# A decoder trunk on one core: the low weight parts of two Conformer layers made by accumulating DMA, with the convolution work divided anew

## The chip, the core and the metric

The kernel runs on one NeuronCore of a Trainium2 chip. A core has a matrix engine (PE, with its weight loads shown apart as PEld), a vector engine (DVE), an activation engine (ACT), a general engine (POOL) and a queue engine (SP) that issues transfers; 16 DMA engines move the data. The five engines run their own instruction lists in order and wait for one another through semaphores. The metric is the device time of one execution in microseconds, lower being better.

## The reference: what is computed

Four residual layers over a sequence of 512 positions with 1024 channels, in the order Conformer, forgetting attention, short convolution, Conformer. Each adds its mixer's output to the stream. Only the two Conformer layers (layer 0 and layer 3) change here:

```python
def conformer_conv_mixer(h, w_in, conv_w, conv_b, ln_g, ln_b, w_out):
    proj = h @ w_in                                  # 1024 -> 3 x 2048
    val, glu_gate, z = jnp.split(proj, 3, axis=-1)
    u = val * jax.nn.sigmoid(glu_gate)
    u = causal_depthwise_conv(u, conv_w) + conv_b    # 31 taps for each of 2048 channels
    u = jax.nn.silu(layer_norm(u, ln_g, ln_b))       # mean and variance over all 2048 channels
    return (u * jax.nn.silu(z)) @ w_out              # 2048 -> 1024
```

The layer norm runs over all channels, so every channel's convolution must be finished before the first value can enter the output projection. All inputs are float32.

## The kernel before

**Precision.** The matmuls run on float32r operands. To keep float32's accuracy each operand is split into a high part (the value cast to float32r) and a low part (the value less its high part), and a product is the sum of three matmuls: high by high, high by low, low by high.

**Weights.** All weights come as 289 chunks of 128x1024 (512 KB). A Conformer layer uses 64: 48 for the input projection (`val`, `gate` and `z` for each of 16 tiles of 128 channels) and 16 for the output projection. For each chunk SP loads `w_raw`, ACT casts it to `w_hi` (L315), and in a Conformer layer POOL subtracts to get `w_lo` (L413); in the output projection DVE may do it too. Three `w_raw` buffers and four pairs of `w_hi` and `w_lo` are in rotation, so the chunk three ahead is prepared while PE works. One chunk is 24 matmuls of 128x512.

**The convolution.** Tile i of u has 31 taps. Tap 0 is an ACT copy into the PSUM tile `cv`. Some taps go to the side: ACT multiplies u by the tap's weight (`prod`, L317) and POOL adds it to `pacc` (L330); `POOL_TAPS` holds how many taps a tile gives away. The rest are DVE instructions (L341, `cv<-u,vt,cv`), one for each tap, each reading the one before. At the end DVE adds `cv`, bias and `pacc` into `d`. Tiles in `PE_TILES` are done by PE instead: ACT reorders u into four phases (`ua`), SP writes it to DRAM (`ud`) and reads it back in four pieces (`phases`), 36 matmuls with banded matrices `pw` give `cv`, ACT copies it (`oa`), SP takes it through DRAM again (`od`, `ob`), and ACT puts it in order into `d`.

**Statistics.** POOL keeps running sums `s1` (of `d`) and `s2` (of its square, `sq`). The last two tiles, 14 and 15, don't go through POOL: PE adds their columns to the sum over channels directly, in PSUM tiles `meanp` and `e2p`. From those come `mean` and `var`, the inverse root `lnrp`, and then for each tile k the gated value (`make_g`: subtract the mean, multiply by `lnrp`, Silu on ACT, multiply by `sz`), split into `g_hi` (ACT) and `g_lo` (DVE). PE's output projection (`o`) takes them two tiles to a chunk.

**Order.** The program registers operations in a list (`Plan`), with a cost for each engine that may run it, and `Plan.trace` simulates the engines by those costs and emits the instructions in the order that comes out; each engine then runs its list in that order. Priorities are the position in the list plus `boost`. The costs are a plan, not measured times. `z` projections are registered nine tiles behind `val` and `gate` (`LAG`), and PE fills its time with them: an order on PE is free of the convolution until the statistics.

```python
POOL_TAPS = (0, 7, 7, 7, 7, 7, 7, 7, 7, 7, 7, 7, 7, 7, 9, 7)
PE_TILES = {0: (7, 12, 15), 3: (7, 12, 15)}
```

**Start.** In layer 0, x arrives in eight pieces, ACT makes `hh` and the squares `sq` of each, PE projects the first four chunks with unnormalised inputs, and sums the squares with a matrix of ones (`ms`); the inverse root `rstd` then gives the normalised `hn` for the other chunks.

Of the kernel before, what the change touches and what calls it, by code (L numbers as in the profile page):

```python
# [16 lines left out]
P = 128  # L17
# [72 lines left out]
class Op:  # L90
    __slots__ = ("engines", "fn", "prio", "table", "deps", "after", "unmet", "ready", "start",
                 "bufs", "new", "urgent")


class Plan:
# [23 lines left out]
    def op(self, engines, fn, r=(), w=(), boost=0, table=None):  # L119

        o = Op()
        o.engines, o.fn, o.prio, o.table = engines, fn, len(self.ops) + boost, table
        o.urgent = boost <= -2000 and "dma" not in engines
# [23 lines left out]
    def trace(self, switch):  # L147
# [25 lines left out]
        for _ in range(len(ops)):  # L173
# [57 lines left out]
            for m in o.after:  # L231
# [3 lines left out]
                if len(p.engines) > 1 or e not in p.engines:  # L235
                    late = self.LATENCY + (self.SLACK if "pe" in p.engines else 0.0)
# [14 lines left out]
def trunk(ctx: ExitStack, tc: tile.TileContext, x, w, vec, pw, out):  # L251
# [38 lines left out]
    def dve_time(n, fast=False):  # L290
        return 0.16 + n * (0.52e-3 if fast else 1.042e-3)
# [111 lines left out]
    def split_chunk():  # L403
# [5 lines left out]
        act(hi, raw, None, cost=1.03, boost=-600)  # L409
# [5 lines left out]
        parts[n] = hi, lo  # L415
        state["split"] += 1
# [26 lines left out]
    memset(ones_d, 1.0 / D)  # L443
    memset(ones_e, 1.0 / E)
# [39 lines left out]
    class Stream:  # L484
# [8 lines left out]
        def add(self, d):  # L493
# [7 lines left out]
            act(sq, xs[d], AF.Square, boost=40 if self.layer == 0 else 0)  # L501
# [24 lines left out]
    def out_projection(layer, gh, gl, make_g, banks):  # L526
# [5 lines left out]
        def evac(d, acc):  # L532
            tt(("dve",), xs[d], acc, xs[d], A.add)
            if last_layer:
                plan.op({"dma": 0.9}, lambda e, d=d: nc.sync.dma_start(out[d], xs[d]()), [xs[d]])
            else:
                nxt.add(d)

# [28 lines left out]
    def conformer(layer, st):  # L567
# [3 lines left out]
        raw_tiles, SPREAD, SHIFTED, DIRECT = 2, 12, 4, 2  # L571
# [3 lines left out]

        s1, s2, m0 = slot("s1"), slot("s2"), slot("m0")
# [34 lines left out]
        def conv_pe(i):  # L611
# [10 lines left out]
            def swap(src, dram, dst):  # L622

                plan.op({"dma": 2.5}, lambda e: nc.sync.dma_start(dram(), src()), [src], [dram], first)
                for k in range(NP):
# [3 lines left out]
                        [dram], [dst], first)  # L629

            plan.op({"act": 0.65}, lambda e: nc.scalar.copy(
                ua()[:, :].rearrange("p (h m) -> p h m", h=NP),
                u()[:, :].rearrange("p (m h) -> p h m", h=NP)), [u], [ua], first)
            swap(ua, ud, r)
            jobs = [(g, lag) for g in range(NP) for lag in range(NL)]
            for k in range(0, len(jobs), 4):
                mats = slot("pw", ring=("pw", 5))
                plan.op({"dma": 0.8}, lambda e, mats=mats, k=k: nc.sync.dma_start(
                    mats(), pw[n if layer == 0 else len(PE_TILES[0]) + n, k // 4]), w=[mats])
# [5 lines left out]
            act(oa, acc, None, boost=first)  # L645
# [396 lines left out]
```

## Time and profile before

| what | value |
|---|---|
| runs shown | 1792.42, 1793.99, 1795.02 us; median 1793.99 |
| the profiled execution | 1794.22 us, of which the trace spans 1792.3 |
| PE | 1767.3 us busy (99%), 8196 matmuls |
| DVE, POOL, ACT | 1167.2 (65%), 1096.9 (61%), 866.7 us (48%) |
| layer 0 | from the start to about 402.7 us |
| layer 3 | from 1400.3 us to the end |
| DMA | 182.4 MB, mean 102 GB/s |

The trace is one execution. Its groups give, for each line, engine and pair of tiles, how many instructions there were, their busy time and mean length, and the idle time just before them with what ended it. Matmuls are pipelined: one matmul's shown length (389 ns) overlaps the next, so PE's speed is read from the start-to-start time of a run of them, in the chain of waits, and a PE that shows as busy may still be waiting inside. An fp32 matmul is recorded as two entries. The share of an engine over the whole span hides that DVE and POOL are loaded in the Conformer layers far above their averages.

### The profile page before, as it was taken

To read this page: it belongs to the slowest core of one execution; us is meant where nothing else is said; L and a number is where in the kernel's file an instruction comes from. 1 tells how busy PE (TensorE), PEld (TensorE's weight loads), DVE (VectorE), ACT (ScalarE), POOL (GpSimd) and SP (SyncE) were. 2 spreads that over 40 slices of the span, in tenths; PEclk is the share of its full clock that TensorE was granted. 3 is DMA by queue.
4 is the path that set the end of the run, shared out by engine and by line. 5 is a ranking of instruction groups with operands and counts; after the bars stand their busy time and mean duration, and the time that the engine had idled before them with its cause. 6 is when DMAs were issued, how large, how long until landed. Compare 5 with 4: busy or idle time off the path is not lost.

```text
span 1792.3 us, 21883 instructions
## 1 busy us (share of the span) xinstructions
PE 1767.3 (99%) x8196; PEld 1462.4 (82%) x8196; DVE 1167.2 (65%) x1690; ACT 866.7 (48%) x1255; POOL 1096.9 (61%) x654
## 2 busy tenths in 40 slices
PE   8999999999999999999999999999999999999999
PEld 6788887888888888888788888888888878878787
DVE  6999997736777777867523333333313699999770
ACT  6656655536555555656433222222223564755550
POOL 5999998865333333544454555455445599989882
PEclk9999999999999999999999999999999999999999
DMA  6243432233222222222222222222223224334222
GB/s 219 83 154 99 141 135 83 94 106 118 83 78 91 85 77 85 75 77 71 71 95 94 94 94 100 101 94 95 96 100 123 88 94 147 106 129 136 94 94 71
DMA packets 63065, 182.40 MB, mean 102 GB/s; under 512 B 7136, under 2 KB 13280, under 8 KB 62960
## 3 DMA queue, kind: packets, MB, share of 16 engines
q1 hardware_dynamic: 62960, 181.02, 29.9%
q8 instruction: 64, 1.05, 0.2%
q14 instruction: 41, 0.34, 0.1%
HBM read 175.71 MB, written 5.28 MB: 101 GB/s over the span
## 4 chain that ended last, share of the span: by engine, by line
PE 81%; DVE 16%; POOL 1%; issue 1%; DMA 1%; ACT 0%; SPq 0%; DVEq 0%; POOLq 0%; ACTq 0%
PE o L379 19%; PE z L379 17%; DVE cv L341 13%; PE k L379 5%; PE v L379 5%; PE u L379 5%; PE c L379 5%; PE b L379 5%; PE q L379 5%; PE gate L379 3%; PE val L379 3%; PE cv L379 2%; PE op L379 2%; PE lg L379 2%; PE pt L874 1%
## 5 line engine op out<-in xcount | busy, mean ns | idle before, releaser
L413 POOL TENSOR_TENSOR w_lo<-w_raw,w_hi 128x1024 fp32r<-128x1024 f32 x274 | 661.1, 2414 | 586.2 <-PE z L379 110.0
L315 ACT CAST w_hi<-w_raw 128x1024 fp32r<-128x1024 f32 x289 | 303.2, 1050 | 550.9 <-issue 137.1
L341 DVE SCALAR_TENSOR_TENSOR cv<-u,vt,cv 128x495 f32<-128x495 f32 (+24 forms) x608 | 447.2, 736 | 19.7
L330 POOL TENSOR_TENSOR pacc<-prod,pacc 128x510 f32<-128x510 f32 (+5 forms) x148 | 174.7, 1181 | 11.1 <-ACT prod L317 4.4
L330 DVE TENSOR_TENSOR x<-o,x 128x512 f32<-128x512 f32 x32 | 21.2, 687 | 200.9 <-PE o L379 200.9
L317 ACT ACTIVATE prod<-u,vt 128x510 f32<-128x510 f32 (+8 forms) x166 | 106.9, 709 | 46.3 <-DVE u L330 46.3
L379 PE MATMUL o<-g_hi,w_hi 128*128 128x512 f32 x512 | 127.9, 391 | 0.7 <-DVE z L330 0.7
L379 PE MATMUL o<-g_lo,w_hi 128*128 128x512 f32 x512 | 127.0, 389 | 0.0
L379 PE MATMUL o<-g_hi,w_lo 128*128 128x512 f32 x512 | 126.7, 389 | 0.0
L379 PEld LDWEIGHTS o<-g_hi,w_hi 128*128 128x128 f32 x512 | 95.8, 188 | 21.7 <-DVE z L330 1.5
L379 PEld LDWEIGHTS o<-g_hi,w_lo 128*128 128x128 f32 x512 | 96.0, 188 | 19.9
L379 PEld LDWEIGHTS o<-g_lo,w_hi 128*128 128x128 f32 x512 | 95.9, 188 | 19.8
L246 ACT ACT_TABLE_LOAD x70 | 89.8, 1283 | 1.9 <-PEq L1030 0.7
L330 DVE TENSOR_TENSOR z<-z,rstd 128x512 f32<-128x512 f32 x32 | 22.1, 691 | 90.2 <-PE z L379 90.1
L379 PE MATMUL z<-hn_hi,w_hi 128*128 128x512 f32 x256 | 65.8, 400 | 2.2 <-ACT sz L317 2.2
L379 PE MATMUL z<-hl,w_hi 128*128 128x512 f32 x256 | 64.6, 394 | 0.0
L379 PE MATMUL z<-hn_hi,w_lo 128*128 128x512 f32 x256 | 64.3, 393 | 0.0
L379 PE MATMUL z<-hh,w_hi 128*128 128x512 f32 x256 | 64.0, 392 | 0.0
L379 PE MATMUL z<-hn_lo,w_hi 128*128 128x512 f32 x256 | 63.7, 391 | 0.0
L379 PE MATMUL z<-hh,w_lo 128*128 128x512 f32 x256 | 63.3, 389 | 0.0
L379 PEld LDWEIGHTS z<-hn_hi,w_hi 128*128 128x128 f32 x256 | 48.1, 191 | 13.9 <-ACT sz L317 3.8
L341 DVE SCALAR_TENSOR_TENSOR hl<-x,vt,hh 128x512 fp32r<-128x512 f32 x32 | 47.6, 1508 | 16.6 <-ACT hh L317 16.6
(245 smaller groups left out, 3708.1 us busy)
## 6 DMA issues: line engine op xcount, KB each, us to landing
w_raw<-w SPq DMA_DIRECT2D x289, 512.0 KB, 3.3
pw<-pw SPq DMA_DIRECT2D x54, 256.0 KB, 4.5
nc<-cd SPq DMA_DIRECT2D x16, 256.0 KB, 3.6
x<-x SPq DMA_DIRECT2D x8, 256.0 KB, 5.2
out<-x SPq DMA_DIRECT2D x8, 256.0 KB, 3.7
ud<-ua SPq DMA_DIRECT2D x6, 256.0 KB, 2.0
phases<-ud SPq DMA_DIRECT2D x24, 64.0 KB, 2.5
od<-oa SPq DMA_DIRECT2D x6, 256.0 KB, 3.9
```

Source lines behind the costliest of these rows:

```text
L246: switch(table)
L315: nc.scalar.copy(of(dst, d), of(src, s))
L317: nc.scalar.activation(of(dst, d), of(src, s), func, **kw)
L330: eng[e].tensor_tensor(of(dst, d), of(a, s), of(b, sb), op)
L341: nc.vector.scalar_tensor_tensor(of(dst, d), of(a, s), c, bb.bitcast(F32) if b_f32r else bb, op0, op1)
L379: nc.tensor.matmul(o, a, b, start=start, stop=stop)
L413: eng[e].tensor_tensor(lo(), raw(), hi().bitcast(F32), A.subtract)
L874: nc.tensor.transpose(tp()[:, blk(i - j)], p[i]()[:, blk(j)], ident())
```

## The change

In chunks 9 to 55 (layer 0) and 234 to 280 (layer 3), 47 in each layer, `w_lo` is made another way: ACT writes the negated high part into `w_lo`, and POOL issues a DMA that reads the weights from DRAM a second time and adds them into `w_lo` in place. After the middle of the output projection the old way is used again. The PE convolution tiles go from 7, 12 and 15 to 8 and 15; the other tiles give 9 taps to POOL instead of 7 (tile 14: 10 instead of 9). Only the last DVE tile (14) is added to the statistics directly by PE; tile 15 now goes through POOL's running sums. The DMAs to DRAM of a PE tile are issued by ACT, right behind its copy, instead of SP. At the start, PE multiplies a matrix of ones by itself 11 times, DVE casts the first chunk, and POOL makes four of the eight squares. In layer 3 each output tile is added and stored in two halves. The planner gets a `lag` for transfers, and `sz` a higher priority.

```diff
+WARM = 11
-POOL_TAPS = (0, 7, 7, 7, 7, 7, 7, 7, 7, 7, 7, 7, 7, 7, 9, 7)
-PE_TILES = {0: (7, 12, 15), 3: (7, 12, 15)}
+POOL_TAPS = (0, 9, 9, 9, 9, 9, 9, 9, 9, 9, 9, 9, 9, 9, 10, 9)
+PE_TILES = {0: (8, 15), 3: (8, 15)}
...
-                    late = self.LATENCY + (self.SLACK if "pe" in p.engines else 0.0)
+                    late = self.LATENCY + o.lag + (self.SLACK if "pe" in p.engines else 0.0)
...
     def split_chunk():
...
-        act(hi, raw, None, cost=1.03, boost=-600)
+        if n == 0:
+            plan.op({"dve": 0.7}, lambda e: nc.vector.tensor_copy(hi(), raw()), [raw], [hi], -600)
+        else:
+            act(hi, raw, None, cost=1.03, boost=-600)
+        parts[n] = hi, lo
+        state["split"] += 1
+        if lo_engines["now"] == ("swdge",):
+            act(lo, hi, AF.Copy, scale=-1.0, cost=1.05, boost=-600)
+            plan.op({"pool": 0.9}, lambda e: nc.gpsimd.dma_start(lo(), w[n], accum_op=A.add),
+                    [hi], [lo], boost=-600, lag=5.5)
+            return
...
+    warm = psum("o", "warm")
+    mms(lambda: [(warm()[:, :P], ones_d(), ones_d(), True, True)] * WARM, [warm], 0.4 * WARM,
+        [ones_d], -3000)
...
-            act(sq, xs[d], AF.Square, boost=40 if self.layer == 0 else 0)
+            if self.layer == 0 and d % 2:
+                tt(("pool",), sq, xs[d], xs[d], A.mult)
+            else:
+                act(sq, xs[d], AF.Square, boost=40 if self.layer == 0 else 0)
...
+            y = [plan.buf(lambda: xs[d]()) for _ in range(2)]
+            for b, s in zip(y, (slice(0, T // 2), slice(T // 2, T))):
+                plan.op({"dve": dve_time(T // 2)}, lambda e, s=s: nc.vector.tensor_tensor(
+                    xs[d]()[:, s], acc()[:, s], xs[d]()[:, s], A.add), [acc, xs[d]], [b])
+                plan.op({"dma": 0.5}, lambda e, s=s: nc.sync.dma_start(
+                    out[d][:, s], xs[d]()[:, s]), [b])
...
+            def phases_out(e):
+                nc.scalar.copy(ua()[:, :].rearrange("p (h m) -> p h m", h=NP),
+                               u()[:, :].rearrange("p (m h) -> p h m", h=NP))
+                nc.scalar.dma_start(ud(), ua())
+            plan.op({"act": 1.05}, phases_out, [u], [ua, ud], first, lag=3.0)
+            swap(ud, r)
...
-            if i < NE - DIRECT:
+            if i != late:
                 tt(("pool",), s1, s1, d2[i], A.add)
                 tt(("pool",), s2, s2, sq, A.add)
...
+            if n == 6:
+                lo_engines["now"] = ("swdge",)
...
-                act(sz[i], acc, AF.Silu)
+                act(sz[i], acc, AF.Silu, boost=-300)
...
-        lo_engines["now"] = ("pool", "dve")
+        lo_engines["now"] = ("swdge",)
 
         def make_g(k):
+            if k == NE // 2:
+                lo_engines["now"] = ("pool", "dve")
```

The new order on two engines, at three places. First POOL's list in the middle of layer 0's convolutions, before (`w_lo23` is chunk 23's low part, `pacc` the running sum of one tile's side taps, `prod` ACT's product for a tap, with the width left by its shift; `m0` is a common offset, `d4` tile 4's result):

```order
L585 COPY pacc_164_1281<-m0_47_665 128x1
L330 TENSOR_TENSOR pacc_164_1281<-prod_165_952,m0_47_665 128x511
L413 TENSOR_TENSOR w_lo23_1292<-w_raw23_1123,w_hi23_1279 128x1024
L330 TENSOR_TENSOR pacc_164_1281<-prod_166_955,pacc_164_1281 128x510
L330 TENSOR_TENSOR pacc_164_1281<-prod_167_961,pacc_164_1281 128x509
L330 TENSOR_TENSOR s1_45_715<-s1_45_715,d4_143_1325 128x512
L330 TENSOR_TENSOR s2_46_717<-s2_46_717,sq_144_1341 128x512
L413 TENSOR_TENSOR w_lo24_1377<-w_raw24_1162,w_hi24_1356 128x1024
L330 TENSOR_TENSOR pacc_164_1281<-prod_168_977,pacc_164_1281 128x508
```

The same stretch of POOL's list now:

```order
L332 TENSOR_TENSOR pacc_175_1265<-prod_176_1098,m0_48_700 128x511
L332 TENSOR_TENSOR pacc_175_1265<-prod_177_1102,pacc_175_1265 128x510
L332 TENSOR_TENSOR pacc_175_1265<-prod_178_1106,pacc_175_1265 128x509
L332 TENSOR_TENSOR pacc_175_1265<-prod_179_1121,pacc_175_1265 128x508
L419 DMA w_lo23_1302<-w 128x1024
L332 TENSOR_TENSOR pacc_175_1265<-prod_180_1136,pacc_175_1265 128x507
L332 TENSOR_TENSOR s1_46_721<-s1_46_721,d4_152_1324 128x512
L332 TENSOR_TENSOR pacc_175_1265<-prod_181_1151,pacc_175_1265 128x506
L332 TENSOR_TENSOR s2_47_723<-s2_47_723,sq_153_1354 128x512
L419 DMA w_lo24_1358<-w 128x1024
```

Each subtraction over a chunk has become a DMA issue at about the same place, and more taps stand between two of them.

Second, PE's list in layer 0 where the statistics are closed, before (`z0_12` is the z projection of tile 12, `d14` and `d15` the last two convolution results; behind the last of the four statistics matmuls there are 80 matmuls of z until the first `o`):

```order
L379 MATMUL z0_12_351_2656<-hn0_7_lo_77_427,w_hi44_2433 128x512
L379 MATMUL meanp_359_2560<-d14_315_2669,ones_e_11_75 128x512
L379 MATMUL e2p_360_2568<-sq_316_2679,ones_e_11_75 128x512
L379 MATMUL meanp_359_2560<-d15_324_2565,ones_e_11_75 128x512
L379 MATMUL e2p_360_2568<-sq_338_2598,ones_e_11_75 128x512
L379 MATMUL z0_12_351_2656<-hn0_0_hi_55_276,w_lo44_2522 128x512
```

And now, with 64 matmuls of z behind it until the first `o`:

```order
L381 MATMUL z0_13_374_2763<-hn0_7_hi_77_411,w_hi45_2588 128x512
L381 MATMUL meanp_380_2784<-s1_46_721,ones_e_11_75 128x512
L381 MATMUL e2p_381_2786<-s2_47_723,ones_e_11_75 128x512
L381 MATMUL meanp_380_2784<-d14_336_2775,ones_e_11_75 128x512
L381 MATMUL e2p_381_2786<-sq_337_2782,ones_e_11_75 128x512
L381 MATMUL z0_13_374_2763<-hn0_0_lo_57_280,w_hi45_2588 128x512
```

The running sums, which PE took 64 matmuls of z earlier before, now stand directly ahead of tile 14, and one third of z tile 13's chunk and all of tile 12's lie before the statistics.

Third, PE's list at the same point of layer 3, where before the four matmuls stood together as in layer 0, again with 80 of z behind them. Now the two that close the statistics are eight matmuls of z apart; the second of them, and the two sides of it:

```order
L381 MATMUL z3_13_1808_14051<-hn3_5_lo_1506_11672,w_hi270_13866 128x512
L381 MATMUL z3_13_1808_14051<-hn3_6_lo_1509_11686,w_hi270_13866 128x512
L381 MATMUL z3_13_1808_14051<-hn3_7_lo_1512_11702,w_hi270_13866 128x512
L381 MATMUL e2p_1815_14034<-sq_1771_14067,ones_e_11_75 128x512
L381 MATMUL z3_13_1808_14051<-hn3_0_hi_1490_11563,w_lo270_13913 128x512
```

Behind it 56 matmuls of z are left until the first `o`.

More of the change, by code (lines that the diff above doesn't have):

```diff
@@ L117, in buf, with op @@
         return b
-    def op(self, engines, fn, r=(), w=(), boost=0, table=None):
+    def op(self, engines, fn, r=(), w=(), boost=0, table=None, lag=0.0):
         o = Op()
         o.engines, o.fn, o.prio, o.table = engines, fn, len(self.ops) + boost, table
+        o.lag = lag
         o.urgent = boost <= -2000 and "dma" not in engines
@@ L414, in split_chunk @@
         plan.op({e: cost[e] for e in lo_engines["now"]}, fn, [raw, hi], [lo], boost=-300)
-        parts[n] = hi, lo
-        state["split"] += 1
     def chunk():
@@ L532, in evac @@
         def evac(d, acc):
[L533 to L536, printed above, removed]
+            if not last_layer:
+                tt(("dve",), xs[d], acc, xs[d], A.add)
                 nxt.add(d)
+                return
+            y = [plan.buf(lambda: xs[d]()) for _ in range(2)]
[4 more added lines that the diff above has]
+                    out[d][:, s], xs[d]()[:, s]), [b])
         accs = [psum(banks[d], f"o{d}") for d in range(half)]
@@ L570, in conformer @@
         FIRST, EARLY = 2, 7
-        raw_tiles, SPREAD, SHIFTED, DIRECT = 2, 12, 4, 2
+        raw_tiles, SPREAD, SHIFTED = 2, 12, 4
         def cw(i, s):
             return v(f"conv_w{layer}", i * KC + KC - 1 - s)
+        late = max(i for i in range(NE) if i not in on_pe)
         s1, s2, m0 = slot("s1"), slot("s2"), slot("m0")
@@ L620, in conv_pe, with swap @@
                       for nm in (f"ud{layer}_{i}", f"od{layer}_{i}"))
-            def swap(src, dram, dst):
-                plan.op({"dma": 2.5}, lambda e: nc.sync.dma_start(dram(), src()), [src], [dram], first)
+            def swap(dram, dst):
                 for k in range(NP):
@@ L638, in conv_pe @@
                 plan.op({"dma": 0.8}, lambda e, mats=mats, k=k: nc.sync.dma_start(
-                    mats(), pw[n if layer == 0 else len(PE_TILES[0]) + n, k // 4]), w=[mats])
+                    mats(), pw[n if layer == 0 else len(PE_TILES[0]) + n, k // 4]), w=[mats],
+                    lag=4.0)
                 mms(lambda mats=mats, k=k: [
@@ L644, in conv_pe, with conv_out @@
                     [acc], 0.87, [mats, r], boost=first or SPREAD * (k // 4))
-            act(oa, acc, None, boost=first)
-            swap(oa, od, ob)
+            def conv_out(e):
+                nc.scalar.copy(oa(), acc())
+                nc.scalar.dma_start(od(), oa())
+            plan.op({"act": 1.05}, conv_out, [acc], [oa, od], first, lag=3.0)
+            swap(od, ob)
             vb, at = v(f"conv_b{layer}", i)
@@ L707, in conformer @@
                 sz[i] = slot(f"sz{i}")
-                act(sz[i], acc, AF.Silu)
+                act(sz[i], acc, AF.Silu, boost=-300)
         mp, ep = psum("o", "meanp"), psum("sum", "e2p")
-        for n, (a, b) in enumerate(zip([s1] + [d2[i] for i in range(NE - DIRECT, NE)],
-                                       [s2] + last)):
+        for n, (a, b) in enumerate(zip([s1, d2[late]], [s2] + last)):
             for dst, src in ((mp, a), (ep, b)):
                 mms(lambda n=n, dst=dst, src=src: [
-                    (dst(), ones_e(), src(), n == 0, n == DIRECT)], [dst], 0.86, [ones_e, src],
+                    (dst(), ones_e(), src(), n == 0, n == 1)], [dst], 0.86, [ones_e, src],
                     boost=-2000)
```

8 lines of the change are left out of this document (2 added, 6 removed).

## The prediction

> **What bounds the kernel now.** The page's first part first, then its chain of what ended last.
>
> ```profile
> PE 1767.3 (99%) x8196; PEld 1462.4 (82%) x8196; DVE 1167.2 (65%) x1690; ACT 866.7 (48%) x1255; POOL 1096.9 (61%) x654
> ```
>
> By this line PE bounds everything. I therefore cut out the stretches that the change touches: start, the convolutions of layer 0, its statistics, the convolutions of layer 3 (columns: stretch, length, busy time of PE, PEld, DVE, ACT, POOL, granted clock, DMA share, GB/s).
>
> ```profile
> 0.00:20.00 20.00, 13.20 (x30) 6.89 (x30) 8.65 (x8) 14.67 (x22) 11.81 (x20) 1.00 0.78 281
> 33.30:291.60 258.30, 253.94 (x1215) 210.90 (x1214) 246.32 (x343) 156.04 (x212) 236.66 (x168) 1.00 0.36 119
> 291.60:316.00 24.40, 24.40 (x102) 18.88 (x101) 15.65 (x23) 16.29 (x22) 17.71 (x12) 1.00 0.22 74
> 1430.00:1683.00 253.00, 247.09 (x1178) 205.42 (x1176) 235.24 (x326) 149.28 (x201) 231.47 (x165) 0.99 0.36 119
> ```
>
> In the convolutions three engines are nearly full: PE 253.9, DVE 246.3 and POOL 236.7 of 258.3. Which one sets the end shows in the groups of that stretch (count | busy, mean ns | idle before, and on whom) and in DVE's waits (us in all, count, longest).
>
> ```profile
> L341 DVE SCALAR_TENSOR_TENSOR cv<-u,vt,cv 128x501 f32<-128x501 f32 (+24 forms) x304 | 223.6, 736 | 9.8
> L341 DVE SCALAR_TENSOR_TENSOR d<-cv,vt,pacc 128x512 f32<-128x512 f32 x12 | 9.0, 750 | 2.0 <-DVE cv L341 0.7 <-POOL pacc L330 0.5
> L413 POOL TENSOR_TENSOR w_lo<-w_raw,w_hi 128x1024 fp32r<-128x1024 f32 x42 | 100.8, 2401 | 8.7 <-ACT w_hi L315 5.3 <-ACT hn_hi L315 2.6 <-issue 0.7
> L330 POOL TENSOR_TENSOR pacc<-prod,pacc 128x510 f32<-128x510 f32 (+3 forms) x74 | 87.3, 1181 | 5.6 <-ACT prod L317 2.4
> L330 POOL TENSOR_TENSOR s<-s,d 128x512 f32<-128x512 f32 x13 | 16.8, 1293 | 6.9 <-DVE d L341 6.7
> L330 POOL TENSOR_TENSOR pacc<-prod,m 128x511 f32<-128x511 f32 x9 | 9.8, 1091 | 0.0
> L317 ACT ACTIVATE prod<-u,vt 128x510 f32<-128x510 f32 (+7 forms) x83 | 53.2, 709 | 25.5 <-DVE u L330 25.5
> L315 ACT CAST w_hi<-w_raw 128x1024 fp32r<-128x1024 f32 x42 | 43.8, 1044 | 27.1 <-issue 14.2 <-PE z L379 8.1 <-PE gate L379 4.0
> ```
> ```profile
> DVE d L341 <- DVE cv L341: 0.7, 2, 0.5
> DVE d L341 <- POOL pacc L330: 0.5, 1, 0.5
> ```
>
> DVE is the bound: 304 taps with 9.8 us of idle before them, 0.03 us each with no releaser named, and almost nothing else that it waits for. PE is full only because z work, free of the convolution, fills it. When DVE's last tap is done the layer goes through statistics, and PE keeps busy with the z that was left over. Four numbers set the length of a Conformer layer: when DVE begins, how long its chain is, how long the last convolution takes to reach the last sum, and how long PE's z lasts behind it.
>
> ```profile
> 22.79 5.44 PE gate L379 x24
> 1648.37 8.03 PE cv L379 x72
> ```
>
> One chunk costs PE 5.44 us (0.2267 for a matmul), one PE convolution tile 8.03.
>
> **The change part by part.** *PE.* One PE tile and two pairs of sums (0.86 for a sum by start to start, below) less: 8.03 + 1.7 = 9.75 us in each layer. In the convolutions this is not on the path by itself. It makes room for 16 and 24 z matmuls ahead of the statistics, whose effect comes below.
>
> *DVE's chain.* Tiles 7 and 12 come to DVE (21 taps each), tile 8 leaves, and two taps of every other tile go to POOL: by the list of instructions 302 taps instead of 304, one more `d`. So -2 x 0.736 + 0.75 = -0.7 in a layer, **-1.4** in both.
>
> *POOL.* 39 passes of 2.40 in the stretch go, 39 DMA issues of unknown cost c come, with 31 more `pacc` adds (1.181), one `prod,m` (1.09), and one running-sum add net (1.29): 236.7 - 93.6 + 36.6 + 1.1 + 1.3 = 182.1 + 39c. No row of before shows c. It lies between SP's issue, in the tail row below (0.33), and POOL's own pass (2.40); I take 1.0, nearer to SP's because an issue touches no data of the tile. POOL then has 221 us of work in 257, less than before; with c up to 1.9 it fits. Cost nothing, then, hidden under DVE's taps.
>
> ```profile
> L366 DVE TENSOR_TENSOR hn_lo<-hn,hn_hi 128x512 fp32r<-128x512 f32 x5 | 3.3, 683 | 0.0
> L366 DVE TENSOR_TENSOR g_lo<-d,g_hi 128x512 fp32r<-128x512 f32 x9 | 13.1, 1477 | 0.1
> w_raw<-w SPq DMA_DIRECT2D x289, 512.0 KB, 3.3
> 1788.63 0.69 DVE L330 TENSOR_TENSOR x<-o,x 128x512 f32<-128x512 f32 x1 [10.19 <-PE o L379]
> 1789.35 0.33 SPq L535 DMA_DIRECT2D out<-x  x1
> ```
>
> A row that speaks for dearer issues: DVE's low parts take 0.68 in the convolutions (`hn_lo`), and 1.48 on average from 300 to 335 us, beside POOL's passes (`g_lo`), so DVE and POOL do hold one another up at times. The Trainium skill, page "SBUF — State Buffer", section "SBUF: two separate sides", warns of just this change: a DMA issued by POOL stalls while DVE runs an instruction that takes both of its ports, since POOL then can't write the descriptors. It limits this to some instructions, and the taps, which read `cv` from PSUM and one tensor from SBUF, are none of them by its words; by it the sum stays, unless the taps count too. No run so far shows a POOL issue.
>
> *The transfer.* A pair of buffers comes free when its chunk ends and its low part is needed three chunks and 16 matmuls later: 3 x 5.44 + 3.63 = 19.9 us. The cast (1.04) and the negation (taken as 1.05) leave 17.8 for issue and landing; loading a chunk takes 3.3. DMA is busy 0.36 at 119 GB/s; 39 chunks of 512 KB in 258 us are 79 GB/s more, share 0.60 at the same rate, 0.84 if adding costs twice. Bounds from 0 to that 0.84: taken at nothing. If it were late, PE's `w_lo` matmuls would wait, 16 z behind them.
>
> *ACT.* 39 negations (1.05) and 32 `prod` (0.64 of busy time each): 156 + 41 + 20 = 217 of 257. It fits; behind ACT stand only casts three chunks ahead and `prod` for a later tile. It is not hidden behind the statistics, below. *SP* loses issues (the `pw` loads of a tile, `ud`, `od`), nothing.
>
> *Start.*
>
> ```profile
> 16.57 1.67 ACT L317 ACTIVATE sq<-x 128x512 f32<-128x512 f32 x3
> 17.67 2.57 PE ms L379 x6
> 20.34 0.69 ACT L317 ACTIVATE rstd<-ms,eps_t 128x512 f32<-128x512 f32 x1 [2.10 <-PE ms L379]
> ```
>
> ACT is the queue that makes `rstd` late: its last squares run to 18.2 and PE's sums to 20.2. It sheds one cast (1.04) and four squares of 0.56, 3.3 us in all, and PE's six pending sums (2.57) partly come earlier. Bounds 0 (the x pieces arrive too late) and -4: taken **-3.0**, all of which shifts DVE's beginning. The ones matmuls I cost at nothing, since PE waits there for ACT (13.2 busy of 20).
>
> *From the last convolution to the first output matmul,* layer 0 above, layer 3 below:
>
> ```profile
> 290.79 0.75 DVE L341 SCALAR_TENSOR_TENSOR d<-cv,vt,pacc 128x512 f32<-128x512 f32 x1 [0.49 <-POOL pacc L330]
> 296.43 1.02 PE L379 MATMUL e2p<-sq,ones_e 128*128 128x512 f32 x2
> 308.39 0.62 ACT L315 CAST g_hi<-d 128x512 fp32r<-128x512 f32 x1 [1.06 <-DVE d L330]
> 310.09 0.62 ACT L315 CAST g_hi<-d 128x512 fp32r<-128x512 f32 x1 [1.08 <-DVE d L330]
> 315.45 1.98 PE L379 MATMUL o<-g_hi,w_hi 128*128 128x512 f32 x8
> 315.82 0.61 ACT L315 CAST g_hi<-d 128x512 fp32r<-128x512 f32 x1
> ```
> ```profile
> 1676.09 0.75 DVE L341 SCALAR_TENSOR_TENSOR d<-cv,vt,pacc 128x512 f32<-128x512 f32 x1 [0.33 <-POOL pacc L330]
> 1682.38 1.02 PE L379 MATMUL e2p<-sq,ones_e 128*128 128x512 f32 x2
> 1701.78 0.62 ACT L315 CAST g_hi<-d 128x512 fp32r<-128x512 f32 x1
> ```
>
> From the end of the last `d` to the end of the last sum it is 5.9 us in layer 0 and 6.5 in layer 3, of which four sums take 3.4 and PE's z ahead of them the rest. With one direct tile it could be 1.75 (the square, 0.63, and a sum of 1.02), in layer 3 some 3.5, since eight z matmuls (1.8) stand between the two. I take half of either gain, because the z ahead may still be under way: **-2.1** and **-1.5**.
>
> Behind the last sum stand 64 and 56 matmuls of z instead of 80: 16 and 24 x 0.2267 = **-3.6** and **-5.4**, if the gated values are there. The first `g_hi` ends 11.6 after the last sum (297.45), the second 13.3 and is needed four matmuls (0.9) after the start of `o`, which is now at 14.5 and 12.7: they just fit. The third ends 19.0 after (316.43 and 1702.40); it is needed a chunk (5.44) after the start of `o`, at 19.9 and 18.1. And ACT now has up to three negations (3.15) ahead of it, where POOL, which also does steps of those tiles, loses passes of 2.4. Bounds 0 to 2.3 in layer 0 and 0 to 4 in layer 3; taken **+1.0** and **+2.5**.
>
> *Tail.* The last output tile in two halves: **-0.2** (from -0.5, half of the 0.69 and a smaller transfer, to +0.3, one more issue).
>
> Sum: -3.0 - 1.4 - 2.1 - 1.5 - 3.6 - 5.4 + 1.0 + 2.5 - 0.2 = -13.7, against the profiled execution's 1794.22: **1780.5**. Its median is 0.23 lower, which I leave out. The bounds of these terms give the main case 1773 to 1790.
>
> **The rivals.** A: PE is the bound after all, as the page's 99% says, and every matmul taken out counts: 1794.2 - 2 x 9.75 - 3.0 - 0.2 = 1771.5. For it: before, PE had just 4.4 us free in 258. Against: DVE's gapless chain.
>
> B: ACT eats it. If all the negations behind the statistics (four, and one in flight, 5.25) stand ahead of a needed `g_hi`, 10.5 more than the sum: 1791. For it: ACT is 16.3 of 24.4 busy there, and the gated values pass it twice. Against: POOL is relieved at the same place.
>
> C, slower: POOL's issue costs over 1.9 and POOL becomes the bound; DVE's `d` waits for `pacc`. Each 0.1 more costs 3.9 in a layer. The gain of 13.7 is used up at c = 2.1; at 2.25, 182.1 + 87.8 = 269.9 against 257, +26 in both, 1806. The Trainium skill's rule above would work in this way if taps counted. For it: the doubled low parts. Against: the taps' steady 0.736 beside a POOL that is 92% busy.
>
> D, slower: the accumulating transfer lands later than 17.8 us. Each us more costs one in four chunks, 94 / 4 = 23 us: 1804. Against: loads land in 3.3.
>
> **How the numbers follow.** Forecast 0.58, A 0.14, B 0.13, C 0.11, D 0.04. The likeliest is 1780.5. The range 1769 to 1796 takes in A and B and leaves out C and D and a little on either side. What this kernel's measurement can tell from no change is 0.2%, 3.6 us. Faster by more: 0.56 of the forecast, A, and 0.05 of B, 0.75; within: 0.02 and 0.07, 0.09; slower: C, D and the last 0.01, 0.16.
>
> **What the profile after would show.** DVE's taps still gapless in the convolutions, with POOL clearly below its 92% (right), or DVE's `d` waiting for `pacc` and POOL at 95% (C). The last square of the start and `rstd` some 3 us earlier. From the last `d` to the last sum 2 to 4 us instead of 6. `o` at about 14.5 and 12.7 behind the last sum, and a gap of a few us behind its first chunk, with ACT's negations ahead of the third `g_hi`. Waits of PE for `w_lo` would show D. The forecast is wrong at the root if DVE waits for `u`, `prod` or `pacc` more than some us, or if PE shows no idle time and the time falls by 20 and more.

## The result, and the profile after

| | before | changed |
|---|---|---|
| median (all runs) | 1794.10 us (1792.42 to 1795.02, 4 runs) | 1784.48 us (1783.39 to 1786.77, 4 runs) |
| ratio | | 0.9945, 95% interval 0.9932 to 0.9957 |
| profiled execution, its span | 1794.22, 1792.3 us | 1784.80, 1783.0 us |

9.6 us faster; forecast were 13.7, at 1780.5 with a range of 1769 to 1796. Three of the four stretches of the trace now, all but the start (columns as in the prediction):

```profile
33.30:291.60 258.30, 252.58 (x1170) 211.48 (x1170) 246.14 (x342) 211.40 (x282) 219.91 (x203) 0.99 0.78 193
291.60:316.00 24.40, 24.40 (x102) 18.87 (x101) 15.78 (x26) 19.34 (x27) 12.77 (x13) 1.00 0.66 150
1430.00:1683.00 253.00, 246.35 (x1135) 202.90 (x1134) 234.25 (x326) 204.29 (x272) 217.26 (x204) 0.99 0.80 193
```

In the convolutions DVE is as full as before, ACT went from 156 to 211 us, POOL from 237 to 220, and the DMA share from 0.36 to 0.78. The groups of 33 to 292 us, and DVE's waits there:

```profile
L343 DVE SCALAR_TENSOR_TENSOR cv<-u,vt,cv 128x498 f32<-128x498 f32 (+22 forms) x302 | 221.7, 735 | 9.8
L332 POOL TENSOR_TENSOR pacc<-prod,pacc 128x510 f32<-128x510 f32 (+4 forms) x105 | 133.0, 1267 | 7.3 <-ACT prod L319 2.0
L319 ACT ACTIVATE w_lo<-w_hi 128x1024 fp32r<-128x1024 f32 x39 | 41.0, 1051 | 4.2 <-PE z L381 2.4 <-PE val L381 0.8 <-ACT prod L319 0.4
L419 POOL DMA_DIRECT2D w_lo<-w x39 | 34.9, 896 | 13.8 <-ACT w_lo L319 13.7 <-issue 0.2
```
```profile
DVE raw L332 <- PE gate L381: 0.7, 1, 0.7
DVE raw L332 <- PE val L381: 0.2, 1, 0.2
DVE d L343 <- DVE cv L343: 0.2, 1, 0.2
```

The taps are still gapless, a POOL issue shows as 0.896 us (I had taken 1.0), and DVE waits for `pacc` no more at all. The adds' longer mean (1267 ns, 1181 before) comes from the adds that follow an issue directly: 25 of them are shown with 1.51 us and overlap the issue's row, the other 80 with 1.19.

The ledger of the two traces follows the layer. It is read from the timeline: the start of the first tap, the end of the last `d`, the end of the last sum (`e2p`), the first `o`, and the first matmul of what follows, or the start of the last output addition.

| step | layer 0: before, changed | difference | layer 3: before, changed | difference |
|---|---|---|---|---|
| first tap starts | 38.30, 39.87 | +1.57 | 1426.22, 1423.79 | (-2.43, carried in) |
| first tap to end of last `d` | 253.24, 252.43 | -0.81 | 250.62, 248.72 | -1.90 |
| to the end of the last sum | 5.91, 5.32 | -0.59 | 6.56, 5.92 | -0.64 |
| to the first `o` | 18.00, 14.37 | -3.63 | 17.99, 12.55 | -5.44 |
| to the layer's end | 87.04, 88.13 | +1.09 | 87.24, 88.42 | +1.18 |

With -0.06 between the layers and -0.15 from the start of the last addition to the end this adds up to the 9.38 us by which the span fell (1792.33 to 1782.95). Two rows differ from the forecast in kind: the start, +1.57 where I had -3.0, and the way from the last `d` to the last sum, -0.6 where I had -2.1 and -1.5.

Which engine came last to the sums shows in PE's first sum over the last `d`, in layer 0 before, changed, and in the first test below (the squares on ACT):

```profile
293.86 1.02 PE L379 MATMUL meanp<-d,ones_e 128*128 128x512 f32 x2
```
```profile
295.74 1.02 PE L381 MATMUL meanp<-d,ones_e 128*128 128x512 f32 x2
```
```profile
287.80 1.13 PE L381 MATMUL meanp<-d,ones_e 128*128 128x512 f32 x2
```

The last `d` ends at 291.54, 292.30 and 287.75. So PE reached this sum 2.3 us behind `d` before and 3.4 us behind it in the changed kernel: `d` lay ready, and PE was the later one. Only in the first test, at 0.05 us, does DVE's chain set the end.

### The profile page after: what moved, and what is told of

Read it like the earlier page. It is cut to its first block, busy times and chain, and to the rows that moved or that the text cites. A ratio compares the mean times of both kernels' runs of the same rounds, so it can differ in the third digit from the quotient of the medians.

```text
span 1783.0 us, 21925 instructions
## 1 busy us (share of the span) xinstructions
PE 1756.1 (98%) x8066; PEld 1452.2 (81%) x8066; DVE 1148.2 (64%) x1695; ACT 983.5 (55%) x1404; POOL 1038.7 (58%) x728
## 5 line engine op out<-in xcount | busy, mean ns | idle before, releaser
L425 POOL TENSOR_TENSOR w_lo<-w_raw,w_hi 128x1024 fp32r<-128x1024 f32 x182 | 439.4, 2415 | 579.2 <-PE z L381 113.3
L343 DVE SCALAR_TENSOR_TENSOR cv<-u,vt,cv 128x493 f32<-128x493 f32 (+22 forms) x604 | 443.5, 735 | 19.5
L332 POOL TENSOR_TENSOR pacc<-prod,pacc 128x510 f32<-128x510 f32 (+4 forms) x210 | 266.1, 1267 | 16.0 <-ACT prod L319 5.5
L319 ACT ACTIVATE prod<-u,vt 128x510 f32<-128x510 f32 (+8 forms) x230 | 153.0, 710 | 4.4 <-DVE u L332 3.5
L332 DVE TENSOR_TENSOR x<-o,x 128x512 f32<-128x512 f32 x24 | 16.0, 687 | 158.3 <-PE o L381 158.3
L419 POOL DMA_DIRECT2D w_lo<-w x94 | 83.2, 885 | 48.6 <-ACT w_lo L319 48.3
L319 ACT ACTIVATE w_lo<-w_hi 128x1024 fp32r<-128x1024 f32 x94 | 98.8, 1052 | 11.0 <-PE z L381 7.3
```

The lines of the kernel that those rows point to most:

```text
L319: nc.scalar.activation(of(dst, d), of(src, s), func, **kw)
L332: eng[e].tensor_tensor(of(dst, d), of(a, s), of(b, sb), op)
L343: nc.vector.scalar_tensor_tensor(of(dst, d), of(a, s), c, bb.bitcast(F32) if b_f32r else bb, op0, op1)
L419: plan.op({"pool": 0.9}, lambda e: nc.gpsimd.dma_start(lo(), w[n], accum_op=A.add), [hi], [lo], boost=-600, lag=5.5)
L425: eng[e].tensor_tensor(lo(), raw(), hi().bitcast(F32), A.subtract)
```

## The experiments

Each was timed beside the kernel before on the same chip, on four chips in all, where the kernel before had medians of 1794.5 to 1795.3; "ratio" is to that kernel, and a difference of a us or two between the medians of two tests isn't read. Where an edit says that an instruction runs on another engine "at the same place", the planner is told the old engine, so that every other instruction keeps its place.

**1. The start: who holds up the inverse root?** In the changed kernel DVE's eight `hl` (x times the norm's weight, less `hh`; both inputs in SBUF) take far longer. The groups of the first 27 us, before and changed:

```profile
L341 DVE SCALAR_TENSOR_TENSOR hl<-x,vt,hh 128x512 fp32r<-128x512 f32 x8 | 8.7, 1140 | 7.0 <-ACT hh L317 7.0
```
```profile
L343 DVE SCALAR_TENSOR_TENSOR hl<-x,vt,hh 128x512 fp32r<-128x512 f32 x8 | 16.3, 2105 | 0.8 <-ACT hh L319 0.8
L425 POOL TENSOR_TENSOR w_lo<-w_raw,w_hi 128x1024 fp32r<-128x1024 f32 x5 | 13.1, 2637 | 6.3 <-PE val L381 3.8 <-DVE w_hi L412 2.5
L332 POOL TENSOR_TENSOR sq<-x 128x512 f32<-128x512 f32 x4 | 5.9, 1485 | 0.0
```

In the trace an `hl` takes 0.74 us alone, 1.52 beside one of POOL's squares and 2.86 beside one of its passes for a low part, and ends some 0.5 us behind POOL's instruction each time; the square then takes 1.49 instead of 1.04, the pass 2.82 instead of 2.4. PE's list needs `hl` in its first chunk, and the next rows of the changed kernel's timeline show what came of it, in matmuls and in the granted clock (third last column) from 24 to 27 us:

```profile
19.79 0.50 PE L381 MATMUL val<-hl,w_hi 128*128 128x512 f32 x1 [1.05 <-DVE hl L343]
22.54 0.50 PE L381 MATMUL val<-hl,w_hi 128*128 128x512 f32 x1 [2.25 <-DVE hl L343]
25.36 2.95 PE L381 MATMUL gate<-hh,w_hi 128*128 128x512 f32 x8
24.00:27.00 3.00, 3.00 (x8) 2.32 (x7) 2.31 (x4) 1.25 (x3) 1.30 (x1) 0.50 0.21 83
```

The first test gives the four squares back to ACT, at the same place:

```diff
-                tt(("pool",), sq, xs[d], xs[d], A.mult)
+                plan.op({"pool": 0.14 + 2.2e-3 * T}, lambda e: nc.scalar.activation(
+                    sq(), xs[d](), AF.Square), [xs[d]], [sq])
```

> The changed kernel with its four POOL squares of the start run by ACT, at the same places of the order; all else as in the changed kernel (profiled execution 1784.8, hl 16.31 us for eight, first tap at 39.87). Theory S (POOL's squares, which read x from SBUF, hold up DVE's hl, and PE's first chunk waits for hl): the eight hl take under 11 us in all, PE's first chunk has no waits of 1 and 2 us for hl, the granted clock stays 1.00 at 24 to 27 us, the first tap comes at 36 to 38 us, and the time falls by 2 to 4 us to 1781 to 1783. Rival W (POOL's passes for the first low parts, which were there before too, hold hl up as much): hl still takes over 14 us, time within 1 us of 1784.5.

Measured: **1777.89 us** (1777.23 to 1778.78), ratio 0.9903 (0.9890 to 0.9916). This is 6.6 us below the changed kernel, more than either theory said, and the lowest median of all kernels here. The start came out as theory S had it, with the first tap at 35.69, just ahead of its 36 to 38 and 2.61 before that of the kernel before:

```profile
L343 DVE SCALAR_TENSOR_TENSOR hl<-x,vt,hh 128x512 fp32r<-128x512 f32 x8 | 8.0, 1057 | 3.4 <-ACT hh L319 3.4
24.00:27.00 3.00, 3.00 (x15) 2.47 (x14) 2.50 (x4) 2.33 (x4) 2.41 (x1) 1.00 0.17 66
```

So the start term was near to right but for the squares' place: 4.18 of the gain over the changed kernel are the first tap. The path to it isn't the one that was forecast, though. `rstd` comes later here than in the changed kernel (18.57, there 17.62); what the changed kernel lost is on PE, whose first chunk waited 1.05 and 2.25 us for `hl` and then ran at the half clock, so that DVE waited 2.06 us for the first `gate`. The rest of the gain is mostly the sums (2.04 behind the last `d` instead of 5.32 in layer 0, 4.28 instead of 5.92 in layer 3), less 3.3 us that this execution lost to the slow clock in the unchanged layers.

The converse is the start alone, put into the kernel before: the first cast on DVE (as in the diff of the change) and the odd squares on POOL, at ACT's places.

```diff
+            if self.layer == 0 and d % 2:
+                plan.op({"act": 0.17 + 0.835e-3 * T}, lambda e: nc.gpsimd.tensor_tensor(
+                    sq(), xs[d](), xs[d](), A.mult), [xs[d]], [sq], 40, ...)
```

> The kernel before, with only the start's division of work changed: DVE casts the first chunk and POOL makes the odd four of the eight squares, at the places in the order where ACT did (no ones matmuls). Theory S (POOL's squares hold up DVE's hl, and with it PE's first chunk): the eight hl take 14 us or more instead of 8.7, the first tap comes 0.5 to 2.5 us later than the 38.30 of before, and the kernel is 0.5 to 3 us slower, 1795 to 1797. My prediction's term: 3.0 faster, 1791.

Measured: 1799.21 us (1798.39 to 1801.24), ratio 1.0027 (1.0016 to 1.0038): slower, as theory S said, and by more. `hl` took 13.4 us (1746 ns each; 14 or more were expected), and the first tap came at 42.53, 4.2 later (0.5 to 2.5 expected). Here a second thing adds to it: in this order the last square stands in POOL's list behind a pass for a low part, and PE waits for it.

```profile
19.58 2.79 POOL L416 TENSOR_TENSOR w_lo<-w_raw,w_hi 128x1024 fp32r<-128x1024 f32 x1
22.32 1.04 POOL L505 TENSOR_TENSOR sq<-x 128x512 f32<-128x512 f32 x1
23.41 1.13 PE L379 MATMUL ms<-sq,ones_d 128*128 128x512 f32 x2 [1.76 <-POOL sq L505]
```

The squares on DVE, at the same place (`nc.vector.tensor_tensor` in the diff of the first test):

> The changed kernel with the four POOL squares of the start made by DVE, at the same places of the order (with them on ACT: first tap at 35.69, 1777.89). ACT is relieved of 4 x 0.56, DVE gets 4 x 0.68 in a stretch in which it waited 2.6 and 2.8 us. Theory S: no contention but with POOL's passes for the low parts; first tap 34.5 to 36.5, 1776 to 1779. Rival (any second instruction with two inputs in SBUF beside hl is as bad, on DVE because it stands in its queue): first tap after 37.5, over 1780.

Measured: 1787.84 us (1784.49 to 1793.32), ratio 0.9965 (0.9953 to 0.9977), first tap at 41.86. The times are the rival's, but its reason isn't enough: the squares cost their 0.68 each, while three `hl` each met one of POOL's passes for a low part, two of which stood back to back, and came out at 2.8 us each. The last square was queued behind them on DVE.

```profile
12.51 8.37 DVE L343 SCALAR_TENSOR_TENSOR hl<-x,vt,hh 128x512 fp32r<-128x512 f32 x3
20.81 0.68 DVE L515 TENSOR_TENSOR sq<-x 128x512 f32<-128x512 f32 x1
15.03 5.31 POOL L425 TENSOR_TENSOR w_lo<-w_raw,w_hi 128x1024 fp32r<-128x1024 f32 x2 [0.21 <-ACT w_hi L317]
21.54 2.08 PE L381 MATMUL ms<-sq,ones_d 128*128 128x512 f32 x2 [5.31 <-DVE sq L515]
```

So it is not the square as such. Whatever POOL does there on tensors in SBUF holds `hl` up, and in the changed kernel the squares filled the gaps between POOL's passes (POOL ran from 5.47 to 21.94 without a pause). The Trainium skill, page "SBUF — State Buffer", section "SBUF: two separate sides", says that a DVE instruction with two SBUF inputs and a POOL instruction that reads SBUF exclude one another for their whole length; these runs agree (0.74 us of `hl` alone, 1.52 and 2.86 beside POOL). I had weighed that section for POOL's DMA issues, which show nothing of the kind, and not for the squares.

Third, the ones matmuls, 1 instead of 11, order unchanged (`* WARM` becomes `* 1`):

> The changed kernel with 1 instead of 11 matmuls of ones at the start, order otherwise unchanged. Theory S: the start is held by hl and not by PE's pace, so the time stays within 1 us of the changed kernel's 1784.5, though the first sums of squares take 0.86 for a record instead of 0.43. Rival (the warm matmuls pay): slower by 2 us or more.

Measured: 1783.17 us (1779.91 to 1789.36), ratio 0.9937 (0.9922 to 0.9953), first tap 39.77 against 39.87. That is 1.3 us from the changed kernel (1 was expected), in executions that lie up to 9 us apart. They cost and bring nothing that can be measured here, as forecast.

**2. PE in the convolutions.** The last run has, behind the start, the changed kernel's list of instructions, and yet its layer 0 closes differently: last `d` at 292.22 (changed: 292.30), last sum at 294.29 (297.62). Two stretches of the changed kernel and then of this run show why, with the PE tile in them:

```profile
149.84 6.33 PE L381 MATMUL cv<-phases,pw 128*128 128x128 f32 x40 [2.78 <-DMA phases<-ud]
262.46 6.33 PE L381 MATMUL cv<-phases,pw 128*128 128x128 f32 x40 [2.94 <-DMA phases<-ud]
264.00:270.00 6.00, 6.00 (x39) 5.77 (x39) 5.72 (x9) 0.00 (x0) 5.69 (x5) 0.81 0.85 238
```
```profile
260.76 4.70 PE L381 MATMUL cv<-phases,pw 128*128 128x128 f32 x40 [1.23 <-DMA phases<-ud]
264.00:270.00 6.00, 6.00 (x40) 5.33 (x39) 5.72 (x9) 1.84 (x2) 5.68 (x5) 1.00 0.83 216
```

The pieces of `phases` land later than before, in the DMA traffic that the accumulating transfers make (the page's list of DMA issues, before and then changed):

```profile
phases<-ud SPq DMA_DIRECT2D x24, 64.0 KB, 2.5
```
```profile
w_lo<-w POOLq DMA_DIRECT2D x94, 512.0 KB, 5.8
phases<-ud SPq DMA_DIRECT2D x16, 64.0 KB, 5.2
```

PE waits nearly 3 us, the granted clock halves for some us (40 entries in 6.33 us instead of 4.70), and PE reaches the sums late. With a wait of 1.23 the clock stays up in this trace and the sums close 2.07 behind the last `d`. In layer 3 the changed kernel's wait ahead of the last PE tile is one for the matrices `pw` (2.14 us), again with the half clock behind it; with the squares on ACT it is 1.43, without.

That the traffic of the accumulating DMAs delays the pieces is borne out by the two tests without these DMAs, which keep ACT's issues for the PE tiles (nine taps with POOL subtracting, under 3, and the test under 6). Their DMA shares are 0.31 and 0.36 from 36 to 290 us, and the pieces land in:

```profile
phases<-ud SPq DMA_DIRECT2D x16, 64.0 KB, 2.9
```
```profile
phases<-ud SPq DMA_DIRECT2D x24, 64.0 KB, 2.8
```

Every run with the accumulating DMAs has 4.1 to 5.3 us there. `pw` goes the same way: 4.0 to 4.5 us without them, 5.3 to 6.7 with them.

The Trainium skill, page "TensorE: Matmul & The Clock Gate", section "Part 1: The HAM clock gate", puts the slow clock down to an idle window of about 3.4 us that runs freely. With a window that runs freely it agrees that the same wait is followed by the slow clock in one execution and not in another: behind PE's wait of 1.9 us in the attention layer the clock is 0.50 with the squares on ACT (749.4 to 752.8 us) and 1.00 in the changed kernel. The length of the wait decides less than that rule says: a wait of 1.36 us was followed by the slow clock (the start alone, 875.6 to 879.0), and one of 3.60 us was not (two direct tiles, 141.8 to 145.4).

To take these waits away, the planner was told a longer landing (with the squares on ACT, as in all tests from here that say so):

```diff
-                        [dram], [dst], first, lag=2.5)
+                        [dram], [dst], first, lag=6.0)
```

> The changed kernel with the squares on ACT (1777.89), and the planner told that the four pieces of `phases` land 6.0 us after their issue instead of 2.5 (in the changed kernel they take 5.2, and PE waits 2.8 and 2.9 us for them in layer 0, behind the first of which the granted clock falls to 0.72 of a 6 us stretch). Theory L (these waits and the slow clock behind them are PE's loss in the convolutions, and they are off the path once the sums close 2.0 us behind the last d, as with the squares on ACT): PE's waits for phases fall under 1 us each, no clock below 0.95 in the convolutions, the time within 1.5 us of 1777.9. Rival (PE is the bound in the convolutions): 3 to 6 us faster, 1772 to 1775.

Measured: 1778.92 us (1777.39 to 1781.03), ratio 0.9912 (0.9899 to 0.9925). One wait of 1.7 us is left in layer 0 (more than the 1 expected), the clock stays at 1.00 in the convolutions, and the time is that of the first test within 1.0. But the planner also put more z ahead of the sums, which now close 5.4 behind the last `d`, with `o` 11.5 behind them: 16.9 in all against 16.4. What PE gained was spent there: with less z left behind the sums it stood idle for the first gated value, 2.40 us in each layer.

```profile
305.43 3.50 PE L381 MATMUL o<-g_hi,w_hi 128*128 128x512 f32 x8 [2.40 <-ACT g_hi L317]
```

Theory L holds for the time; the test doesn't hold all else fixed.

**3. What bounds the convolutions.** Three PE tiles as before, nine side taps:

```diff
-PE_TILES = {0: (8, 15), 3: (8, 15)}
+PE_TILES = {0: (7, 12, 15), 3: (7, 12, 15)}
```

> The changed kernel with PE convolution tiles 7, 12 and 15 as before (13 tiles with nine side taps on DVE, 281 taps a layer instead of 302). PE gets 8.03 us back in each layer, DVE loses 21 x 0.76 + 0.75 = 16.7. Theory D (DVE's chain sets the end of the convolutions, PE has some 5 us free in 258): the convolutions end some 5 to 10 us earlier but the z that PE could not do meanwhile is left behind the statistics, so that the layer ends by PE's work: slower by 2 to 6 us in a layer, 1788 to 1797. Rival A of the prediction (PE is the bound, no slack at all): 2 x 8.03 = 16 slower, 1800. If DVE alone counted: 33 faster.

Measured: 1796.64 us (1794.69 to 1798.68), ratio 1.0008 (1.0000 to 1.0017), at the upper end of theory D's range, 6.1 us in a layer, and not far from rival A's 1800. The last `d` of layer 0 comes at 282.37, 9.9 earlier, and the last sum at 299.51, 17.1 behind it: PE is late. With 8 us more on PE it is PE that sets the end. From the first tap to the last sum it is 259.5 us, in the kernel before 259.2, though DVE's chain was 10.9 us longer there. So with three PE tiles the shorter chain on DVE brought nothing; with the two tiles DVE sets the end where PE's waits are short, as with the squares on ACT.

Ten side taps instead of nine, squares on ACT (`POOL_TAPS` 10, tile 14: 11):

> The changed kernel with the squares on ACT and ten side taps for each tile instead of nine (tile 14: eleven). DVE loses 14 x 0.735 = 10.3 us in each layer, POOL gets 14 x 1.267 = 17.7 more (222 of 258 becomes 240 of 248), ACT 9. Theory D (DVE's chain sets the end of the convolutions): the last d comes 7 to 10 us earlier in each layer, but PE, which has some 4 us to spare there, leaves more z behind the statistics, so that only 2 to 5 us in a layer remain: 1768 to 1774. Rival P (POOL, with its adds at 1.27 and not 1.18, becomes the bound): DVE waits for pacc, 1777 to 1785.

Measured: 1789.02 us (1781.46 to 1792.35), ratio 0.9966 (0.9952 to 0.9979): DVE waits for `pacc`, as in rival P, and the time is worse than its range. The rows of the last `d` in layer 0 and of one of POOL's issues ahead of it:

```profile
293.28 0.75 DVE L343 SCALAR_TENSOR_TENSOR d<-cv,vt,pacc 128x512 f32<-128x512 f32 x1 [13.80 <-POOL pacc L332]
273.54 0.88 POOL L419 DMA_DIRECT2D w_lo<-w  x1 [6.21 <-ACT w_lo L319]
```

That POOL has no room for ten is only part of it. POOL itself stood 6.2 us ahead of that issue, for a negation that stands in ACT's list behind the copy of a PE tile; that tile had waited for `pw` and run at the half clock. Without this stop the last `d` would end at about 288 us (an estimate from the two rows), where nine taps have it (287.75). So the tenth tap gains nothing in layer 0 even then.

And nine taps without the accumulating DMA:

```diff
-            if n == 6:
-                lo_engines["now"] = ("swdge",)
...
-        lo_engines["now"] = ("swdge",)
+        lo_engines["now"] = ("pool", "dve")
```

> The changed kernel without its accumulating DMAs: POOL subtracts for the low parts, as before (in the output projection DVE may do it too), all else as changed, nine side taps among it. POOL gets 37 x 2.40 instead of 37 x 0.90 in the stretch of 258 us: 219.6 + 55.5 = 275. Theory (the accumulating DMA buys the two side taps, and without it POOL is the bound): DVE waits for pacc, slower than 1784.5 by 12 to 22 us in each layer, 1808 to 1828. Rival (POOL has room by its adds running faster, 1.18, without the DMA traffic): 1785 to 1800.

Measured: 1878.99 us (1876.01 to 1879.90), ratio 1.0468 (1.0454 to 1.0481). That DVE waits for `pacc` is right, the size isn't: 47 us in a layer where I expected 12 to 22. POOL is busy 232 of the 254 us from 36 to 290, so the order in which the engines wait for one another adds to POOL's work; by how much is open. From 300 to 420 us DVE waits for `pacc` three times and PE for the running sums, and once z is used up PE stands still; the granted clock from 324 to 342 us is 0.50.

```profile
DVE d L343 <- POOL pacc L332: 34.4, 3, 16.9
PEld meanp L381 <- POOL s L332: 22.0, 1, 22.0
```

**4. The statistics.** The sums over tile 14 ahead of those over the running sums:

```diff
-zip([s1, d2[late]], [s2] + last)
+zip([d2[late], s1], last + [s2])
```

> The changed kernel with the sums over tile 14 ahead of the sums over the running sums in the statistics (the planner moves a few matmuls with them). In the changed kernel the last d ends at 292.30 and the last sum at 297.62 in layer 0, 5.3 us, where I had taken 3.8. Theory R (the four sums stand together behind PE's z, whatever their order, because the running sums of tile 15 come as late as tile 14): still 4.5 to 6 us there, time within 1.5 us of 1784.5. Rival (the running sums, behind which tile 14 stands, are what is late): the last sum 1.5 to 3 us earlier in each layer, 1780 to 1782.

Measured: 1784.98 us (1782.25 to 1787.48), ratio 0.9943 (0.9931 to 0.9955): no change of the time, as theory R said. Its reason doesn't hold, though. The distance from last `d` to last sum was 3.8 in layer 0 (4.5 to 6 expected) and 8.2 in layer 3, where the planner put z between. The 3.8 are not to be set against the changed kernel's 5.3, in which PE's waits and the slow clock are contained; where PE comes in time, the old order closes at 2.07 (without the ones matmuls), with the running sums taken 1.5 us before `d` ends. So the running sums are not as late as tile 14, and ahead of it they are in the better place.

Two direct tiles again, squares on ACT (the condition `i != late` becomes `i < NE - 2`, and the sums take `s1`, tiles 14 and 15):

> The changed kernel with the squares on ACT, and tiles 14 and 15 both added to the statistics directly by PE, as before the change. Theory R (one direct tile saves two sums of 0.86 behind the last d, and the running sums come in time): the last sum 1.7 us later behind the last d than with one (2.04 in layer 0, 4.28 in layer 3), time 1778 to 1782. Rival (the running sums wait for tile 15 on POOL and hold up the end as much): no difference over 1 us.

Measured: 1783.79 us (1779.92 to 1792.95), ratio 0.9948 (0.9928 to 0.9969). In the trace the last sum comes 3.77 and 6.05 behind the last `d`, against 2.04 and 4.28 with one direct tile: 1.73 and 1.77 more. In layer 0 that is just two sums, as theory R had it; in layer 3 the order of z differs too (no z between the closing sums, 63 instead of 55 behind them), so that the same number there is chance. The median is above its 1778 to 1782. Its executions scatter with their mean granted clock, from 1779.92 at 0.999 to 1792.95 at 0.993, so the time by itself says little here.

**5. The output projection.** The third `g_hi` ahead of later chunks' casts and negations, squares on ACT:

```diff
-            boost = -2500 + 10 * k if first else 0
+            boost = -2500 + 10 * k if first else -700 + 10 * k if k < 4 else 0
```

> The changed kernel with the squares on ACT (1777.89), and the steps of the gated values of tiles 2 and 3 given priority over the casts and negations of later chunks, so that on ACT two casts and two negations less stand ahead of the third and fourth g_hi. Theory G (the output projection's loss of 1.1 us in each layer, 88.1 instead of 87.0 from its first matmul to the next layer, is ACT's negations ahead of the third g_hi): no wait of PE for the third g_hi, 87.0 to 87.4 us for that stretch, the time 1.5 to 2.5 us shorter, 1775.4 to 1776.4. Rival (the third gated value is late by POOL's or DVE's steps, and the casts that now come later hold PE up instead): 1777 to 1780.

Measured: 1782.91 us (1779.50 to 1784.48), ratio 0.9932 (0.9918 to 0.9945): no gain, rather slower than the first test. In the changed kernel (first two rows) PE's wait is not for the third `g_hi`, which is ready 0.04 us before its need, but for the fourth, needed four matmuls later; a negation stands right ahead of it in ACT's list. This wait is gone, and one for the sixth stands a chunk later in its place (last row, of this test); the stretch in layer 0 stays at 88.3 us. So ACT's work in these chunks costs the 1.1 us, not its order, or another engine's step of the later tiles; this isn't separated. Its other executions were slower than the profiled one (1779.50), most at a lower mean granted clock (0.994 and 0.995 in the three slowest, 0.997).

```profile
317.68 1.06 ACT L319 ACTIVATE w_lo<-w_hi 128x1024 fp32r<-128x1024 f32 x1 [0.29 <-ACT g_hi L317]
319.30 1.20 PE L381 MATMUL o<-g_hi,w_hi 128*128 128x512 f32 x4 [0.65 <-ACT g_hi L317]
```
```profile
316.48 1.19 PE L381 MATMUL o<-g_hi,w_hi 128*128 128x512 f32 x4 [0.46 <-ACT g_hi L317]
```

**6. All but the new division.** No accumulating DMA, three PE tiles, seven side taps, squares on ACT (the edits above together):

> The changed kernel without the accumulating DMAs (POOL subtracts as before), with the three PE tiles and seven side taps of before; what remains of the change is the cast on DVE, the ones matmuls, ACT's issues for the PE tiles, one direct tile, the halves at the end, and the squares stay on ACT. Theory T (the gain over the squares on POOL and the gain by accumulating DMA and new division add up: from 1777.9 one takes the 16 to 24 matmuls of z and the PE tiles back): start 2.6, sums 3 to 4, tail 0.1 faster than before: 1786 to 1790. Rival N (the start alone moves PE's z as well): 1782 or less. Rival O (the start and the sums are hidden under PE's work, which is then as in the kernel before): 1792 to 1795.

Measured: 1791.32 us (1788.02 to 1793.84), ratio 0.9986 (0.9977 to 0.9995), between theory T and rival O. The first tap comes at 35.67, 2.6 earlier than before; but the last `d` waits 5.8 for `pacc` and the last sum closes 8.8 behind it, so that at the end of layer 0 nothing is left (402.72 against 402.49). Layer 3 is 3.7 us shorter from its first tap to the end. The early start is worth little without the accumulating DMA and the division that it allows: together they bring some 13 to 15 us more (1791.3 to 1777.9, or 0.9986 to 0.9903 of the kernel before).

## Why the prediction was right, and where not

- **DVE's chain as the bound** held only in part. The chain was forecast at -0.7 in each layer and came at -0.81 and -1.90 (layer 3's extra 1.2 wasn't pursued), still gapless. But gapless taps don't show that an engine is the later one at the end: PE reached the sum over the last `d` 2.3 us behind it before and 3.4 us behind it in the changed kernel (layer 0). DVE sets the end only where PE's waits are short (the squares on ACT). Rival A was wrong in its sum, less so in its engine.
- **The start** is the step that failed in sign: "ACT is the queue that makes `rstd` late", -3.0. ACT did get free (`rstd` at 17.62 instead of 20.34), but I costed the four squares on POOL at nothing, with no cover named, and looked only at the queue that they left. On POOL they slowed DVE's `hl` from 1.14 to 2.1 us each, PE's first chunk waited for them, and `nt`, DVE's next step behind `rstd`, came at 22.41 instead of 21.73. With the squares on ACT the term is -2.61, near to the forecast, but only 1.8 of it is `rstd` (18.57 instead of 20.34); the rest came behind it, where one step of DVE had taken 2.77 us beside a pass of POOL before. So the nearness is in part luck.
- **From the last `d` to the last sum**: -2.1 and -1.5 forecast, -0.6 in both. I had left `phases` at 2.5 us when I took the DMA share up to 0.78 (within my 0.60 to 0.84): the transfer was "taken at nothing" for the low parts, where that is right (landing 5.8 of 17.8 us, the longest 8.9, no wait for `w_lo`), and not looked at for the others in the same traffic, `phases` in layer 0 and `pw` in layer 3. Where PE comes in time (the run without ones matmuls; the squares on ACT) layer 0 has 2.07 and 2.04, a gain of 3.8 or 3.9, more than the half that I took.
- **z behind the sums**: -3.6 and -5.4 forecast, -3.63 and -5.44 measured; the gated values just fit, as worked out.
- **The stall behind the first chunk**: +1.0 and +2.5 forecast, +1.09 and +1.18 measured. The mechanism is the one forecast, one tile later: the third `g_hi` just fits, and the fourth, which I hadn't looked at, is late behind ACT's negation.
- **Rivals.** B didn't show. C was refuted by the issue of 0.896 us, though a `d` that waits for `pacc` is near: it comes with the tenth tap. D was refuted by the landing. **Tail**: -0.15 for -0.2.

Both misses ate gain: 4.6 us at the start and 2.4 at the sums; layer 3's chain and its smaller stall gave 2.5 back, which was luck.

## What to carry to other kernels

Work moved off a late queue must be priced on the engine that takes it and on that engine's neighbour: an instruction of POOL on SBUF tensors beside DVE instructions with two SBUF inputs isn't free, even on an idle POOL. New DMA traffic is to be checked against every small round trip in the same stretch, not only against its own deadline. And where several engines are within a few per cent, the gain of one change ends at the next of them (here 8 us more on PE made PE the bound, and one more tap of each tile on POOL made DVE wait for it), so look for the division before the speed-up. Which engine is the later one is read where they meet, from how long the finished input lies before it is used, and not from gapless work alone.

## What was not expected of the hardware

The granted clock falls to one half after PE waits of as little as 1.36 us, for some 3.4 us at a time (0.50 from 24 to 27 us in the changed kernel), in some executions and not in others at the same wait, and not after every wait of 3.6 us. Such drops, in the unchanged layers too, go with most of the scatter: of the kernel with two direct tiles, 13 us between mean clocks of 0.999 and 0.993. The changed kernel's executions have mean clocks of 0.993 to 0.996, those of the kernel before, beside the tests, 0.997 to 1.000. Two of the changed kernel's slow stretches, at the start and ahead of the sums, are part of the gain that was missed. Differences of one or two us between kernels are therefore read from the ledger of a trace rather than from a median.
